# Swapping q and k on ScalarE, and the rows of 1/rms by a transpose through DRAM, in a one-core hybrid layer

## The chip, the cores and the metric

The kernel runs on one core of one Trainium2 chip. The metric is the device time of one execution in microseconds (us); the median of several executions counts. The engines are TensorE (PE, matmuls), VectorE (DVE, elementwise), ScalarE (ACT, activations and copies), GpSimd (POOL, not used here) and SyncE (SP), whose queue issues nearly all transfers (DMA).

## The reference

One layer over 1024 positions of width 1024, in float32. Cut to what matters here:

```
h = rms_norm(x, norm1_w)                       # x * 1/rms(x) per position, times a weight per channel
q, k, v, g_ret, x_lru, y_lru, gate_ret, gate_lru = split(h @ w_in)
q, k = rotary(q), rotary(k) * dk**-0.5         # 4 heads of 128; halves (x1, x2) ->
                                               #   (x1 cos - x2 sin, x1 sin + x2 cos)
o    = chunkwise_retention(q, k, v)            # decayed attention per chunk, state across chunks
y_a  = (head_group_norm(o) * silu(g_ret)) @ w_ret_o
y_b  = (rg_lru(conv(x_lru)) * gelu(y_lru)) @ w_lru_o
x    = x + (sigmoid(gate_ret) * y_a + sigmoid(gate_lru) * y_b) @ w_out
h    = rms_norm(x, norm2_w)
gate, val = split(h @ ffn_w_up)
x    = x + (gelu(conv(gate)) * val) @ ffn_w_down
out  = rms_norm(x, norm_f_w)
```

## The kernel before

All large products run on PE as 128 by 128 by 512 matmuls. Each float32 operand is split into a high part (a cast on ScalarE, L771) and a low part (a subtraction on VectorE, L772), and three products of the parts are added up. Most products of two 1024-wide matrices go through a fast scheme with seven block products in place of eight (`mm_fast`): three PSUM banks X, Y, Z take twelve matmuls per block product (L898), and between the block products ScalarE copies banks (L905, L919) and VectorE adds them up (L910). Twelve matmuls after a bank is full PE may need it again.

The layer runs in stages on PE: the values of all heads first (L1500), then 20 products of the input projection in the order of `SEQ` (gates, y, heads, x), then the output projections of both branches, `w_out` (`out_job`), 24 products of the gated MLP (`up_job`), and `w_dn` in three groups (`down_job`). Activations lie transposed: channels on partitions, positions along the free dimension.

**Retention.** When the product that makes q and k of a head is done, `rotary_head` and `retention_head` are queued behind it as side work that is woven into the next products. `rotary_head` holds k or q as `t`, 128 partitions (channels of the head) by 1024 positions. Rotation needs each channel's partner 64 partitions away: two transfers (L1318, L1319) write the upper half of `t` to the lower half of `w` (tile `qs`) and the lower half to the upper. Then VectorE makes `t*cos` (L1320), `w*sin` (L1321) and the sum (L1323). Keys are then transposed through DRAM (L1327 to L1335). `retention_head` makes per block of 128 positions the scores (L1356), the masked scores times values (L1363), the state's part (L1362) and the state's update (L1370), all on PE in plain float32.

**Rows of 1/rms.** The sum of squares is made per position with positions on partitions: eight columns of 128 positions. `rstd_of` makes 1/rms of them (128 by 8). Since activations lie transposed, 1/rms is needed along the free dimension, on all partitions: the tile `rowt` (128 by 1024). `rows_of` makes it: VectorE scales the identity by a column (L1083), PE multiplies a matrix of ones with that diagonal (L1084), four such per PSUM bank, and ScalarE copies the bank to half of `rowt` (L1085). It is called twice: at the start for the first norm, where `rescale` (L1095) multiplies the input with the row, and after `w_out` for the second norm, where `with_row` (L1416) multiplies each result of an up product with it.

**The order of the work.** All operations are first recorded. A planner then runs through them with a table of costs (`cost`, `forward`), picks for each engine what to run next, and gives tiles their places in SBUF. `side` marks PE work to be woven in, `within(slack, side)` gives a due time. Operations get a random bias from `SEED`; the planner goes through several `ROUNDS`, in each of which it brings forward what held up PE (`blame`), and keeps the order with the shortest planned span. `emit` writes each engine's instructions in that order, so every engine runs a fixed sequence and waits in it. Transfers are planned with a landing time from `TILE` and `LAND`.

Of the kernel before, what the change touches and what calls it, by code (L numbers as in the profile page):

```python
# [17 lines left out]
ALU = mybir.AluOpType  # L18

P = 128  # L20
D = 1024
T = 1024
KT = 8
# [240 lines left out]
class Prog:  # L264
# [378 lines left out]
    EAGER = 12000  # L643
    EARLY = 20000
    FETCH = 24000
    SEED, JITTER, ROUNDS, STALL, URGE = 19, 400.0, 6, 150.0, 6000.0
    BEGIN = 400
    TILE = 800.0
    LAND = 1900.0
# [8 lines left out]
    def emit(self, engines, make, behind):  # L658
        at, sent = {}, []
        for o in self.order:  # L660
# [16 lines left out]

SMALL = (("par", (P, NPAR)), ("cst", (P, NCONST)), ("st", (P, 16)), ("nst", (P, 7, 8)), ("lt", (P, 2, 8)),
         ("state0", (P, 256)), ("state1", (P, 256)), ("bst", (P, 4, 6)),
         ("mv", (P, 4, 2)), ("rs", (P, 3, 4)), ("rowt", (P, T)))  # L680
SPILL = (("og", (KT, P, T)), ("u", (KT, P, T)), ("y", (KT, P, T)), ("sg", (2, KT, P, T)), ("t1", (KT, P, T)),
         ("x1", (T, D)), ("td", (3, 4, 2, P, 2, TH)), ("to", (2, 4, 2, P, 2, TH)), ("ff", (3, 8, P, 2, 4, P)), ("rot", (4, P, T)),
         ("ss", (12, 2, P, T)), ("v", (2, KT, P, TH)),
         ("kt", (HEADS, 2, 4, P, P)), ("ot", (HEADS, 2, 4, P, 2, P)))
# [21 lines left out]
TSLACK = 8000.0  # L706
# [24 lines left out]
def record(prog, fx):  # L731
    V, S, G, PE, SY = (Engine(prog, n) for n in ("DVE", "ACT", "POOL", "PE", "SP"))
    par, cst, st, nst, lt = (fx[n] for n in ("par", "cst", "st", "nst", "lt"))
    rst, bst, mv, rs = fx["rst"], fx["bst"], fx["mv"], fx["rs"]
    og_d, u_d, y_d, sg_d, t1_d, x1_d, td_d, to_d, ff_d, rot_d, ss_d, v_d, kt_d, ot_d = (
        fx[n + "_d"] for n in ("og", "u", "y", "sg", "t1", "x1", "td", "to", "ff", "rot", "ss", "v", "kt", "ot"))
    x, positions, normf, w_in, w_v, w_ro, w_lo, w_out, w_up, w_dn, w_gate, out, xt = (
        fx[n] for n in ("x", "positions", "normf", "w_in", "w_v", "w_ro", "w_lo", "w_out", "w_up", "w_dn", "w_gate", "out", "xt"))
    ident = cst[:, C_ID:C_ID + P]

    def get(name, shape=(P, TH), dt=F32):
        return Ref(VT("u", shape, dt, name))

    def sm():
        return Ref(VT("sm", (P, P), F32, "sc"))

    def bank(kind="g"):
        return Ref(VT(kind, (P, TH), F32, kind))

    def pc(name, i):  # L750
        return par[:, PCOL[name] + i:PCOL[name] + i + 1]

    def cut(t, h):
        if h is None:
            return t
        return t[:, h] if len(t.shape) == 3 else t[:, TH * h:TH * h + TH]
# [4 lines left out]
    @contextmanager  # L761
    def within(slack, side=False):
        was = prog.slack, prog.side
        prog.slack, prog.side = slack, side
        yield
        prog.slack, prog.side = was

    def split(src, name, here=False):
        hi = get(name + "h", src.shape, F32R)
        lo = src.alias(F32R) if here else get(name + "l", src.shape, F32R)  # L770
        S.copy(hi, src)  # L771
        V.tensor_sub(lo, src, hi.bitcast(F32))  # L772
        return hi, lo
# [228 lines left out]
    def put(op, name, jp, made):  # L1002
        for i in range(2):
            op[name, 2 * jp + i] = made[0][:, i], made[1][:, i]
# [65 lines left out]
            V.scalar_tensor_tensor(t2, t2, -1.0, b21, ALU.mult, ALU.subtract)  # L1070
            put(op, "T4", jp, split(t2, "b", True))

    row = {0: fx["rowt"]}

    def rows_of(r, side, slack=1000.0):
        one = sm()
        V.memset(one, 1.0)
        for h in range(2):
            with within(slack, side):
                ps = bank()  # L1080
                for t in range(4):
                    dg = sm()
                    V.tensor_scalar(dg, ident, r[:, 4 * h + t:4 * h + t + 1], None, ALU.mult)  # L1083
                    PE.matmul(ps[:, 128 * t:128 * t + 128], one, dg, start=True, stop=True)  # L1084
                S.copy(cut(row[0], h), ps)  # L1085

    def scaled_split(t, w, name):
        hi, lo = get(name + "h", t.shape, F32R), get(name + "l", t.shape, F32R)
# [4 lines left out]
    def rescale(q, ch, name):  # L1093
        t = q[ch // 2][:, ch % 2]
        V.scalar_tensor_tensor(t, t, pc(name, ch), row[0].rearrange("p (h c) -> p h c", h=2), ALU.mult, ALU.mult)  # L1095

    def start_transposed():
        if UNI:
            q = {(kh, h, jp): get("xq", PAIR) for h in range(2) for kh in range(2) for jp in range(2)}
            for h in range(2):  # L1100
                for k in range(KT):
                    t = q[k // 4, h, k % 4 // 2][:, k % 2]
                    SY.dma_start(t, xt[h, k])
                    S.activation(t, t, AF.Copy, scale=pc("norm1_w", k))
                    b = f"B{k // 4 + 1}{h + 1}"
                    if b != "B12" or STD_L:
                        h1[b, k % 4] = split(t, "h")
            for jp in range(2):
                b11, b12, b21, b22 = (q[kh, h, jp] for kh in range(2) for h in range(2))
                V.tensor_sub(b11, b11, b12)  # L1110
                V.tensor_sub(b12, b22, b12)
                V.scalar_tensor_tensor(b22, b11, -1.0, b22, ALU.mult, ALU.subtract)
                V.scalar_tensor_tensor(b21, b22, -1.0, b21, ALU.mult, ALU.subtract)
                for n, t in (("T1", b11), ("T2", b22), ("T3", b12), ("T4", b21)):
                    put(h1, n, jp, split(t, "b", True))
        q = [get("xq", QUAD) for _ in range(0 if UNI else 4)]
        for h in range(0 if UNI else 2):
            for k in range(KT):
                t = q[k // 2][:, k % 2, h]
                SY.dma_start(t, xt[h, k])  # L1120
                h1u[f"B{k // 4 + 1}{h + 1}", k % 4] = scaled_split(t, pc("norm1_w", k), "h")
        prog.floor = FLOOR1
        for t in range(8):
            b = get("xs", FLAT)
            SY.dma_start(b, x[128 * t:128 * t + 128, :])
            S.activation(b, b, AF.Square, accum_out=nst[:, 0, t:t + 1])
        a, r, w = (nst[:, i, 0:8] for i in range(3))
        V.tensor_scalar(a, a, 1.0 / D, EPS, ALU.mult, ALU.add)
        rstd_of(r, a, w)
        rows_of(r, True)  # L1130
        if not UNI:
            for k in (0, 1, 4, 5, 2, 3, 6, 7):
                rescale(q, k, "norm1_w")
            operand(h1, of_quads(q), ("B11", "B21", "B22"), False)
            tsets(h1, of_quads(q))
        prog.floor = -1e9
# [173 lines left out]
    def rotary_head(hd, qk):  # L1310
        for m in range(2):
            if m == 0 or UNI:
                tab = [get("rt", FLAT) for _ in range(2)]
                for i in range(2):
                    SY.dma_start(tab[i], rot_d[2 * m + i])
            t = qk[m]
            w = get("qs", FLAT)
            SY.dma_start(w[0:64, :], t[64:128, :])  # L1318
            SY.dma_start(w[64:128, :], t[0:64, :])  # L1319
            V.tensor_mul(t, t, tab[0])  # L1320
            V.tensor_mul(w, w, tab[1])  # L1321
            yield 1.8
            V.tensor_add(t, t, w)  # L1323
            yield 1.8
        for h in range(2):
            t = get("kx")
            V.transpose(t.view(lambda a: a.rearrange("p (c b j) -> p c b j", c=4, b=4)),  # L1327
                        cut(qk[1], h).view(lambda a: a.rearrange("p (b c j) -> p c b j", b=4, c=4)))
            SY.dma_start(kt_d[hd, h].rearrange("c p r -> p c r"), t.rearrange("p (c r) -> p c r", c=4))
            yield 0.9  # L1330
            t, kd[h] = get("kl"), get("kd")
            for c in range(4):
                SY.dma_start(t[32 * c:32 * c + 32].rearrange("i (a r) -> i a r", a=4),
                             kt_d[hd, h, c].rearrange("(a i) r -> i a r", a=4))
            S.activation(kd[h].rearrange("p (b a j) -> p b a j", a=4, b=4), t.rearrange("p (a b j) -> p b a j", a=4, b=4),  # L1335
                         AF.Copy, scale=cst[:, C_KDEC + hd:C_KDEC + hd + 1])
            yield 0.5
# [102 lines left out]
    og, u = {}, {}  # L1440
# [86 lines left out]
    for what in SEQ.split():  # L1527
        if what == "g":
            w, n = gates.pop(0)
            to = store(lambda m, w=w, n=n: sg_d[w, 2 * n + m])  # L1530
# [5 lines left out]
        elif what[0] == "y":  # L1536
            n = int(what[1])
            to = store(lambda m, n=n: y_d[2 * n + m])
# [4 lines left out]
        elif what[0] == "x":  # L1543
            n = int(what[1])
# [9 lines left out]
    one, ps = warm = sm(), bank()  # L1554
# [3 lines left out]
        PE.matmul(ps[:, 0:P], one, one, start=True, stop=True)  # L1558
    prog.side = False
    V.memset(st, 1.0)  # L1560
    S.activation(st[:, 0:1], st[:, 1:2], AF.Sqrt)
    prog.hold = 14000.0
    SY.dma_start(par[:, 8:NPAR], fx["params"][:, 8:NPAR])
# [150 lines left out]
    for h in range(2):  # L1714
# [10 lines left out]
        with within(TSLACK, True):  # L1725
            a, b, c, e = (nst[:, i, 4 * h:4 * h + 4] for i in range(4))
            v, r = nst[:, 5, 4 * h:4 * h + 4], nst[:, 4, 4 * h:4 * h + 4]
# [5 lines left out]
                V.tensor_add(v, v, e)  # L1733
            V.tensor_scalar(v, a if RELOAD else v, 1.0 / D, EPS, ALU.mult, ALU.add)
            rstd_of(r, v, a)
    rows_of(nst[:, 4, :], True, max(1000.0, TSLACK))
    if UNU:
        pass
    elif UNS:
# [3 lines left out]
    else:  # L1743
        for h in range(2):
            for k in range(KT):
                t = x1q[k // 2][:, k % 2, h]
# [109 lines left out]
def tile_trunk_layer(ctx, tc, x, positions, params, consts, normf, w_in, w_v, w_ro, w_lo,  # L1856
# [9 lines left out]
    fx["rst"] = [fx.pop("state0"), fx.pop("state1")]  # L1866
    for n, shape in SPILL:
        fx[n + "_d"] = Ref(Fixed(pdr.tile(list(shape), F32, tag=n, name=n + "_d"), shape))
# [83 lines left out]
```

## Time and profile before

| | us |
|---|---|
| three runs | 1582.25, 1582.71, 1580.74 |
| median | 1582.25 |
| the profiled execution, in all | 1582.89 |
| its span | 1581.1 |
| PE busy in the span | 1567.7 |

The profile comes from one execution. Its span runs from the first to the last instruction; the time of the execution is 1.8 us longer. Instructions are named by engine, line of the kernel and tile ("out<-in"). The end of a matmul is modelled and overlaps the next one, so its time on PE is best read as the distance from one start to the next. "[1.24 <-DVE ub L1323]" behind an instruction means that its engine stood idle for 1.24 us before it, and that the instruction on L1323 of VectorE ended this wait.

### The profile page before, as it was taken

Reading aid. Unit: us, or ns where it says so; the run is one execution under the profiler, and the core shown is the slowest. Engines: PE = TensorE matmul, PEld = TensorE weight load, DVE = VectorE, ACT = ScalarE, POOL = GpSimd, SP = SyncE. Lnnn points to the kernel's source line nnn. Section 1 sums busy time; section 2 is a strip of 40 time slices with the busy share of each in tenths; the row PEclk is TensorE's granted clock in tenths of the full one; section 3 lists DMA queues with packets and bytes.
Section 4 is the critical chain, followed back from the end, with each engine's and each line's share of the span. In section 5 each row is a group of like instructions: output and inputs, shape, how many; then the busy total and the mean of one; then the engine's idle time right before and its main releaser. Section 6 shows DMA issues by size and latency. Waiting matters only on the chain.

```text
span 1581.1 us, 19113 instructions
## 1 busy us (share of the span) xinstructions
PE 1567.7 (99%) x6988; PEld 1297.5 (82%) x6988; DVE 1280.9 (81%) x1725; ACT 868.5 (55%) x1171; POOL 0.2 (0%) x4
## 2 busy tenths in 40 slices
PE   9999999999999999999999999999999999999998
PEld 7888888788888888888888888888888888888886
DVE  4996877887888988978795887788888788877795
ACT  7464458476458458645456854444444445454463
POOL 0000000000000000000000000000000000000000
PEclk9999999999999999999999999999999999999999
DMA  9414445457487868959353522456655335776752
GB/s 328 143 65 154 118 157 167 147 178 255 118 296 240 271 209 303 393 205 363 122 178 124 183 80 81 133 187 200 200 195 200 138 100 175 281 269 264 274 198 78
DMA packets 146013, 307.09 MB, mean 194 GB/s; under 512 B 11264, under 2 KB 60544, under 8 KB 145920
## 3 DMA queue, kind: packets, MB, share of 16 engines
q1 hardware_dynamic: 145488, 305.35, 56.4%
q8 instruction: 55, 0.90, 0.2%
q10 hardware_dynamic: 432, 0.53, 0.1%
q14 instruction: 38, 0.31, 0.1%
HBM read 208.31 MB, written 93.32 MB: 191 GB/s over the span
## 4 chain that ended last, share of the span: by engine, by line
PE 91%; DMA 4%; DVE 3%; ACT 1%; issue 1%; SPq 1%; DVEq 0%; ACTq 0%
PE g L898 82%; PE g L1500 4%; PE a L1275 3%; DMA xq<-xt 1%; DMA qs<-ub 1%; PE a L1363 1%; PE a L1362 1%; PE a L1370 1%; DMA qs<-ua 1%; DMA xs<-x 1%; DVE qs L1321 1%; PE a L1680 0%; PE a L1356 0%; DVE wl L772 0%; DVE ub L1323 0%
## 5 line engine op out<-in xcount | busy, mean ns | idle before, releaser
L898 PE MATMUL g<-bh,wh 128*128 128x512 f32 x1728 | 676.0, 391 | 0.6 <-DVE ub L910 0.6
L898 PEld LDWEIGHTS g<-bh,wh 128*128 128x128 f32 x1728 | 324.5, 188 | 68.1 <-DVE ub L910 1.5
L898 PE MATMUL g<-bh,wl 128*128 128x512 f32 x880 | 344.5, 391 | 0.0
L898 PE MATMUL g<-bl,wh 128*128 128x512 f32 x864 | 339.5, 393 | 0.0
L898 PE MATMUL g<-bh,wrr 128*128 128x512 f32 x824 | 321.6, 390 | 0.0
L771 ACT CAST wh<-wr 128x1024 fp32r<-128x1024 f32 (+1 forms) x220 | 198.1, 917 | 102.2 <-PE g L898 28.5
L898 PEld LDWEIGHTS g<-bh,wl 128*128 128x128 f32 x880 | 165.3, 188 | 33.9
L898 PEld LDWEIGHTS g<-bl,wh 128*128 128x128 f32 x864 | 162.3, 188 | 32.9
L772 DVE TENSOR_TENSOR wrr<-wr,wh 128x1024 fp32r<-128x1024 f32 (+1 forms) x154 | 152.0, 990 | 37.5 <-ACT wh L771 37.4
L898 PEld LDWEIGHTS g<-bh,wrr 128*128 128x128 f32 x824 | 154.7, 188 | 31.8
L898 PE MATMUL g<-tdr,wh 128*128 128x512 f32 x320 | 124.5, 389 | 0.0
L771 ACT CAST wh<-ws 128x1024 fp32r<-128x1024 f32 x66 | 69.2, 1049 | 82.6 <-PE g L898 47.0
L898 PE MATMUL g<-hl,wh 128*128 128x512 f32 x288 | 112.2, 390 | 0.0
L898 PE MATMUL g<-hh,wh 128*128 128x512 f32 x288 | 112.1, 389 | 0.0
L910 DVE TENSOR_TENSOR ub<-ub,g 128x512 f32<-128x512 f32 x72 | 49.2, 683 | 53.0 <-PE g L898 52.9
L905 ACT ACTIVATE ub<-g 128x512 f32<-128x512 f32 x72 | 42.8, 596 | 84.0 <-PE g L898 75.6
L772 DVE TENSOR_TENSOR wl<-ws,wh 128x1024 fp32r<-128x1024 f32 x66 | 80.4, 1219 | 9.8 <-PE g L898 9.5
L772 DVE TENSOR_TENSOR wl<-wr,wh 128x1024 fp32r<-128x1024 f32 x66 | 80.3, 1217 | 7.6 <-ACT wh L771 2.7
L898 PE MATMUL g<-tsr,wh 128*128 128x512 f32 x208 | 81.2, 390 | 0.0
L919 ACT ACTIVATE g<-g 128x512 f32<-128x512 f32 x72 | 42.0, 584 | 61.1 <-PE g L898 60.9
L905 ACT ACTIVATE ua<-g 128x512 f32<-128x512 f32 x72 | 43.0, 598 | 56.3 <-PE g L898 52.2
L910 DVE TENSOR_TENSOR ua<-ua,g 128x512 f32<-128x512 f32 x72 | 49.2, 683 | 29.2 <-PE g L898 28.4
(265 smaller groups left out, 2539.1 us busy)
## 6 DMA issues: line engine op xcount, KB each, us to landing
wr<-w_up SPq DMA_DIRECT2D x50, 512.0 KB, 4.5
wr<-w_in SPq DMA_DIRECT2D x48, 512.0 KB, 4.5
dw<-w_dn SPq DMA_DIRECT2D x42, 512.0 KB, 4.6
ff_d<-gc SPq DMA_DIRECT2D x24, 512.0 KB, 3.8
wr<-ff_d SPq DMA_DIRECT2D x24, 512.0 KB, 6.9
td<-td_d SPq DMA_DIRECT2D x24, 512.0 KB, 7.2
x<-x_d SPq DMA_DIRECT2D x24, 512.0 KB, 6.8
td_d<-dw SPq DMA_DIRECT2D x18, 512.0 KB, 5.7
```

What stands on the lines that cost most here:

```text
L771: S.copy(hi, src)
L772: V.tensor_sub(lo, src, hi.bitcast(F32))
L898: PE.matmul(ps, (hi, lo)[a][:, c], o[b], start=first and n == 0, stop=n == 11, skip_group_check=True)
L905: S.activation(cut(d[m], h), ps, AF.Copy, scale=scale)
L910: (V.tensor_sub if m else V.tensor_add)(u, u, ps)
L919: S.activation(Y, X, AF.Copy)
L1275: PE.matmul(ps, wg[a][:, g, cs], xs[b][:, k], start=q == 0, stop=q == 5)
L1321: V.tensor_mul(w, w, tab[1])
L1362: PE.matmul(p2[:, 0:256], q[:, bs], rst[cur], start=True, stop=False)
L1363: PE.matmul(p2[:, 0:256], s, v, start=first, stop=True)
L1370: made.append(PE.matmul(p3[:, 0:256], kd[h][:, bs], v, start=True, stop=True))
L1500: PE.matmul(ps[t], a[i][:, 128 * t:128 * t + 128], b[j], start=k == 0 and i + j == 0, stop=k == KT - 1 and i == 1)
```

## The change

`rotary_head` makes the swapped tile by two copies on ScalarE, each of 64 partitions by 1024, in place of two transfers, and gives back control to the weaving once more. `rows_of` no longer uses PE: VectorE copies 1/rms into the first eight columns of a 128 by 32 tile (`rcol`, whose other columns are zeroed once at the start), transposes it in blocks of 32 by 32 into `rrow`, four transfers store eight rows each of 32 values to a row in DRAM, and one transfer reads that row back to all 128 partitions of `rowt`. Two small tiles and one DRAM buffer are new. The planner gets another seed and one more round.

```diff
-    SEED, JITTER, ROUNDS, STALL, URGE = 19, 400.0, 6, 150.0, 6000.0
+    SEED, JITTER, ROUNDS, STALL, URGE = 6, 400.0, 7, 150.0, 6000.0
...
-         ("mv", (P, 4, 2)), ("rs", (P, 3, 4)), ("rowt", (P, T)))
+         ("mv", (P, 4, 2)), ("rs", (P, 3, 4)), ("rowt", (P, T)),
+         ("rcol", (P, 2, 32)), ("rrow", (P, 2, 32)))
...
-    def rows_of(r, side, slack=1000.0):
-        one = sm()
-        V.memset(one, 1.0)
-        for h in range(2):
-            with within(slack, side):
-                ps = bank()
-                for t in range(4):
-                    dg = sm()
-                    V.tensor_scalar(dg, ident, r[:, 4 * h + t:4 * h + t + 1], None, ALU.mult)
-                    PE.matmul(ps[:, 128 * t:128 * t + 128], one, dg, start=True, stop=True)
-                S.copy(cut(row[0], h), ps)
+    def rows_of(r, side, at):
+        with within(None, side):
+            V.tensor_copy(rcol[:, at, 0:8], r)
+            V.transpose(rrow[:, at], rcol[:, at])
+            for a in range(4):
+                SY.dma_start(row_d[at].view(lambda d, a=a: d.rearrange("o (t a j) -> a (o t) j", a=4, j=32)[a], T // 4),
+                             rrow[32 * a:32 * a + 8, at])
+            SY.dma_start(row[0], row_d[at].to_broadcast((P, T)))
...
-        rows_of(r, True)
+        rows_of(r, True, 0)
...
             w = get("qs", FLAT)
-            SY.dma_start(w[0:64, :], t[64:128, :])
-            SY.dma_start(w[64:128, :], t[0:64, :])
+            S.copy(w[0:64, :], t[64:128, :])
+            S.copy(w[64:128, :], t[0:64, :])
+            yield 1.0
             V.tensor_mul(t, t, tab[0])
             V.tensor_mul(w, w, tab[1])
...
+    V.memset(rcol, 0.0)
...
-    rows_of(nst[:, 4, :], True, max(1000.0, TSLACK))
+    rows_of(nst[:, 4, :], True, 1)
```

More of the change, by code (lines that the diff above doesn't have):

```diff
@@ L679 @@
          ("state0", (P, 256)), ("state1", (P, 256)), ("bst", (P, 4, 6)),
-         ("mv", (P, 4, 2)), ("rs", (P, 3, 4)), ("rowt", (P, T)))
-SPILL = (("og", (KT, P, T)), ("u", (KT, P, T)), ("y", (KT, P, T)), ("sg", (2, KT, P, T)), ("t1", (KT, P, T)),
+         ("mv", (P, 4, 2)), ("rs", (P, 3, 4)), ("rowt", (P, T)),
+         ("rcol", (P, 2, 32)), ("rrow", (P, 2, 32)))
+SPILL = (("row", (2, 1, T)), ("og", (KT, P, T)), ("u", (KT, P, T)), ("y", (KT, P, T)), ("sg", (2, KT, P, T)), ("t1", (KT, P, T)),
          ("x1", (T, D)), ("td", (3, 4, 2, P, 2, TH)), ("to", (2, 4, 2, P, 2, TH)), ("ff", (3, 8, P, 2, 4, P)), ("rot", (4, P, T)),
@@ L734, in record @@
     rst, bst, mv, rs = fx["rst"], fx["bst"], fx["mv"], fx["rs"]
-    og_d, u_d, y_d, sg_d, t1_d, x1_d, td_d, to_d, ff_d, rot_d, ss_d, v_d, kt_d, ot_d = (
-        fx[n + "_d"] for n in ("og", "u", "y", "sg", "t1", "x1", "td", "to", "ff", "rot", "ss", "v", "kt", "ot"))
+    row_d, og_d, u_d, y_d, sg_d, t1_d, x1_d, td_d, to_d, ff_d, rot_d, ss_d, v_d, kt_d, ot_d = (
+        fx[n + "_d"] for n in ("row", "og", "u", "y", "sg", "t1", "x1", "td", "to", "ff", "rot", "ss", "v", "kt", "ot"))
     x, positions, normf, w_in, w_v, w_ro, w_lo, w_out, w_up, w_dn, w_gate, out, xt = (
@@ L1071, in tsets @@
             put(op, "T4", jp, split(t2, "b", True))
-    row = {0: fx["rowt"]}
-    def rows_of(r, side, slack=1000.0):
-        one = sm()
-        V.memset(one, 1.0)
-        for h in range(2):
-            with within(slack, side):
-                ps = bank()
-                for t in range(4):
-                    dg = sm()
-                    V.tensor_scalar(dg, ident, r[:, 4 * h + t:4 * h + t + 1], None, ALU.mult)
-                    PE.matmul(ps[:, 128 * t:128 * t + 128], one, dg, start=True, stop=True)
-                S.copy(cut(row[0], h), ps)
+    row, rcol, rrow = {0: fx["rowt"]}, fx["rcol"], fx["rrow"]
+    def rows_of(r, side, at):
[6 more added lines that the diff above has]
+            SY.dma_start(row[0], row_d[at].to_broadcast((P, T)))
     def scaled_split(t, w, name):
```

## The prediction

> **What bounds the kernel now.** First the page: its head and the busy shares.
>
> ```profile
> span 1581.1 us, 19113 instructions
> PE 1567.7 (99%) x6988; PEld 1297.5 (82%) x6988; DVE 1280.9 (81%) x1725; ACT 868.5 (55%) x1171; POOL 0.2 (0%) x4
> ```
>
> TensorE (PE) is busy 99% of the span, so the end is set by how many matmuls it has and by the few places where it stands. A busy share hides small gaps, because the end of each matmul is modelled; therefore I go on with the windows (columns: stretch, then PE, PEld, DVE, ACT, POOL busy, granted clock, DMA share, GB/s).
>
> ```profile
> 41.00:97.00 56.00, 56.00 (x249) 46.37 (x248) 54.28 (x64) 26.93 (x33) 0.00 (x0) 1.00 0.27 94
> 154.00:200.00 46.00, 45.82 (x212) 38.18 (x211) 36.38 (x79) 21.34 (x35) 0.00 (x0) 1.00 0.49 129
> 272.00:313.00 41.00, 39.63 (x182) 32.55 (x181) 36.77 (x69) 18.72 (x30) 0.00 (x0) 1.00 0.53 151
> 387.00:440.00 53.00, 51.76 (x238) 42.97 (x237) 44.65 (x89) 22.37 (x36) 0.00 (x0) 1.00 0.53 154
> 511.00:562.00 51.00, 50.15 (x229) 41.50 (x229) 46.27 (x82) 21.53 (x34) 0.00 (x0) 1.00 0.78 259
> 608.00:822.00 214.00, 214.00 (x946) 177.24 (x945) 187.06 (x212) 120.41 (x146) 0.00 (x0) 1.00 0.72 268
> 920.00:1574.00 654.00, 654.00 (x2886) 541.47 (x2884) 526.37 (x623) 312.94 (x416) 0.00 (x0) 1.00 0.52 181
> ```
>
> From 608 to 822 and from 920 to 1574 us PE has no gap at all and the clock is full: 654.00/2886 = 0.227 us per matmul of 512 columns. Nothing can be gained there; a new order of work can only lose. The four short windows are those of the four retention heads, and there PE is missing 0.18, 1.37, 1.24 and 0.85 us. Who it waits for stands in the view of waits, PE alone (total, times, longest):
>
> ```profile
> PE a L1356 <- DVE ua L1323: 1.4, 3, 1.0
> PE a L1356 <- DVE ub L1323: 1.2, 1, 1.2
> PE a L1680 <- DVE x1q L1620: 0.8, 1, 0.8
> PE g L898 <- DVE ub L910: 0.6, 1, 0.6
> ```
>
> L1356 is the first score matmul of each head, and L1323 the last step of the rotation of k or q, behind the swap. So the swap stands on the path that sets the end, but only through 2.6 us of waits.
>
> **The matmuls that go.** Two calls of `rows_of` make eight diagonal matmuls each (L1084). What one costs is read from the starts in PE's timeline:
>
> ```profile
> 912.22 0.39 PE L898 MATMUL g<-hh,wrr 128*128 128x512 f32 x1
> 912.44 0.39 PE L898 MATMUL g<-hh,wh 128*128 128x512 f32 x1
> ...
> 913.12 0.40 PE L898 MATMUL g<-hh,wh 128*128 128x512 f32 x1
> 913.36 0.83 PE L1084 MATMUL g<-sc,sc 128*128 128x128 f32 x6
> 913.94 0.48 PE L898 MATMUL g<-hl,wh 128*128 128x512 f32 x1
> 914.26 0.39 PE L898 MATMUL g<-hh,wrr 128*128 128x512 f32 x1
> ```
>
> Each L1084 matmul is two records, so "x6" is three. From 913.12 to 914.26 pass 1.14 us, in which two ordinary matmuls would take 0.45; the rest, 0.69, is three diagonal ones with the way in and out, 0.23 each. All 16 make 16 x 0.23 = **3.7 us**, on the path, since PE is full on both sides. With less lost in changing over it would be 3.4, with single ones 0.26 each, so 4.2: those are the bounds. Their 16 scalings on VectorE and four copies on ScalarE go too; neither ends a wait of PE in the rows above, so they count nothing.
>
> **The swap.** Sixteen transfers go; sixteen ScalarE copies of 64 partitions by 1024 come. First what the transfers cost:
>
> ```profile
> 404.34 0.39 PE L898 MATMUL g<-bl,wh 128*128 128x512 f32 x1
> 405.97 0.71 PE L1356 MATMUL a<-ua,ub 128*128 128x128 f32 x4 [1.24 <-DVE ub L1323]
> ...
> 532.08 0.71 PE L1356 MATMUL a<-ua,ub 128*128 128x128 f32 x4 [0.30 <-DVE ua L1323]
> ```
>
> ```profile
> 520.46 1.23 DVE L1321 TENSOR_TENSOR qs<-qs,rt 128x1024 f32<-128x1024 f32 x1 [2.62 <-DMA qs<-ua]
> ...
> 527.35 0.68 DVE L910 TENSOR_TENSOR ub<-ub,g 128x512 f32<-128x512 f32 x1
> ```
>
> ```profile
> DMA to landing us min/median/max: 3.1/6.7/8.7
> ```
>
> The last row is the view of tile qs: a swap lands 6.7 us after its issue. VectorE works in a fixed order, stands 2.62 us at 520 for it, and the late L910 behind it is the fourth PE wait above (0.6). Waits shown as 1.24 are longer from start to start: 405.97 - 404.34 - 0.23 = 1.40, so 0.16 is hidden in each. Swap-related loss: 1.4 + 1.2 + 0.6 + 5 x 0.16 = **4.0 us** in five stalls.
>
> A copy on ScalarE is priced by the nearest cast of 1024 columns:
>
> ```profile
> L771 ACT CAST wh<-ws 128x1024 fp32r<-128x1024 f32 x66 | 69.2, 1049 | 82.6 <-PE g L898 47.0
> L919 ACT ACTIVATE g<-g 128x512 f32<-128x512 f32 x72 | 42.0, 584 | 61.1 <-PE g L898 60.9
> ```
>
> 1.05 us, half the partitions or not; between 0.53 (if halves cost half) and 1.05 I take 1.05. A pair is 2.1 us in place of 6.7, so a rotated tensor is ready some 4.6 us sooner, and SP's queue loses 16 issues, which stood ahead of weight and value loads. In the four head windows ScalarE gets 4.2 us more on 21.34 of 46, 18.72 of 41, 22.37 of 53 and 21.53 of 51: over 20 us stay free in each, and that is the cover at which I price the copies at nothing.
>
> How much of the 4.0 goes? The planner that writes the order will place the scores earlier as well, because it knows the copies' length. What is then late next is VectorE: three operations of 1.2 us for each of q and k, among weight splits. The wait of 0.30 at 532 follows such a chain. I let one stall of that kind stay per head, 4 x 0.4 = 1.6, and take **-2.4**. Bounds: -4.0 (all gone) and 0 (what is late next takes their place).
>
> **The rows through DRAM.** New at each call: a copy and a 32-wide transpose on VectorE, four small stores, and, after them, one load of 4 KB to all 128 partitions, 512 KB, all on SP's queue.
>
> ```profile
> kt_d<-kx SPq DMA_DIRECT2D x8, 256.0 KB, 2.8
> rt<-rot_d SPq DMA_DIRECT2D x8, 512.0 KB, 3.7
> nf<-normf SPq DMA_DIRECT2D x1, 512.0 KB, 8.6
> ```
>
> ```profile
> 45.53 2.48 DVE L1095 SCALAR_TENSOR_TENSOR xq<-xq,par,rowt 128x1024 f32<-128x1024 f32 x2
> ```
>
> ```profile
> 909.07 0.15 DVE L1000 TENSOR_TENSOR nst<-nst 128x4 f32<-128x4 f32 x1
> ...
> 918.27 1.23 DVE L1416 TENSOR_TENSOR ua<-ua,rowt 128x1024 f32<-128x1024 f32 x1 [1.24 <-ACT rowt L1085]
> ...
> 922.01 0.68 DVE L910 TENSOR_TENSOR ua<-ua,g 128x512 f32<-128x512 f32 x1
> ```
>
> ```profile
> 35.35 0.16 DVE L1000 TENSOR_TENSOR nst<-nst 128x8 f32<-128x8 f32 x1
> ```
>
> ```profile
> 914.22 0.80 SPq L786 DMA_DIRECT2D wr<-w_up  x2
> ```
>
> Second call: 1/rms is ready at 909.2; 0.5 for copy and transpose (an estimate from 0.15 for small operations), four issues of 0.40 = 1.6, the store 2.8 and an issue 0.4 give 914.5. The load then takes 3.7 (same size, plain) or 8.6 (same shape, but one sample): the row lands between 918.2 and 923.1, against its first use at 918.27. So VectorE stands 0 to 4.8 us in front of L1416, and behind it wait L910, which frees a bank for PE, the gate convolution (L1756) and weight splits. PE needs the bank of L910 no sooner than twelve matmuls after it is full, 12 x 0.227 = 2.7 us. On PE that is 0 to 2.1; I take 0.5, nearer the lower end because the load of the same size is the median of eight. On SP the next issue is the load at 914.22, just when the row's load would go: no delay. First call: 35.5 + 0.5 + 1.6 + 2.8 + 0.4 + 3.7 to 8.6 = 44.5 to 49.4, against 45.53. VectorE may stand 3.9 us there, but that is covered:
>
> ```profile
> 97.02 62.57 PE g L898 x276
> ```
>
> ```profile
> 137.75 1.11 SPq L1226 DMA_DIRECT2D rot_d<-rot  x2
> ```
>
> The first products with scaled operands start at 97 (chain of waits), and VectorE's filler until then, the rotary tables, is stored only at 137 (SP's timeline). So 0 is taken, and 3.9 if that cover is gone.
>
> The Trainium skill, page "DMA: Bandwidth & Descriptors", section "Anatomy of one DMA", gives another price and speaks against a way through DRAM: about 2.0 us fixed for each transfer, most of it the receipt of the write, worst where the target is DRAM, and two here stand in series. It is measured on the other kind of queue. The 2.8 above agrees in kind. By its formula the store is 2.0 and the load 3.2 (estimates), the row would be there at 916.9, nothing would wait, and the sum below would be 0.5 lower.
>
> **The other order.** A new seed and one more round of the planner give every engine another order and every tile another place. The stall at L1680 (0.8 shown, 0.94 from start to start) may go: lower bound -0.9. Upper bound: a new stall like the largest, 1.4, in four places, +5.6. No row shows it; I take +0.3, near nothing, since PE is gapless for 868 us in the two long windows with the same kinds of work.
>
> **Sum.** -3.7 - 2.4 + 0.5 + 0.3 = **-5.3 us**. The profiled execution has a span of 1581.1 and took 1582.89 in all; it would be 1577.6. It lies 0.64 above the median of the three runs, 1582.25, so for the median **1577.0**.
>
> **The rivals.**
>
> *All swap stalls go and the row is in time.* For it: 4.6 us sooner is over three times the longest stall, 1.4. Against it: VectorE is 80% busy. 1582.25 - 3.7 - 4.0 = 1574.5. Chance 0.2.
>
> *A wait in place of the one removed.* The keys still go through DRAM for their transpose, 2.8 us and a load behind it, and scores start earlier; PE then stands for the decayed keys or for VectorE as long as now. Only the matmuls go: 1582.25 - 3.7 + 0.5 + 0.3 = 1579.4, with one more 1.4 stall 1580.8. For it: the stalls are named by VectorE, not by the transfer. Chance 0.26.
>
> *ScalarE blocks the bank evictions: slower.* The copies stand in ScalarE's order between evictions such as L919, whose bank PE needs 2.7 us later. A pair of copies and an eviction are 2.1 + 0.58 = 2.7: it just fits. The same stretch also has a table load:
>
> ```profile
> 162.95 1.28 ACT L1234 ACT_TABLE_LOAD   x1
> ```
>
> Where both come ahead of an eviction PE stands about 1.2 us; in all eight pairs that is 9.9: 1582.25 - 3.7 - 2.4 + 9.9 = 1586.1. It decides for slower once all eight pairs are hit (over 6.1 + 3.2 = 9.3), or six of them if the -2.4 isn't had. For it: copies wait for VectorE's L910, in order. Against it: ScalarE is under half busy there and the planner knows all durations. Chance 0.12; some 0.02 is left for new stalls of the order alone.
>
> *The change does not do what it says:* a swap across partitions by copies may run slower than the cast, up to twice (2.1 each). Still a pair of 4.2 lies under 6.7; this falls into the second rival.
>
> **Chances and range.** Forecast 0.40. A measurement of this kernel can tell about 0.2%, 3.2 us: faster is below 1579.1, slower above 1585.4. The forecast counts 0.34 faster and 0.06 same; the first rival 0.2 faster; the second 0.08 faster, 0.18 same; the third 0.02 same and 0.10 slower, the rest 0.02 slower: faster 0.62, same 0.26, slower 0.12. The lower bounds together give 1582.25 - 4.2 - 4.0 - 0.9 = 1573.1; I go to 1572.5. Upwards the second rival with a late row (+1.6 more) and two new stalls (2.8) is 1579.4 + 4.4 = 1583.8; I go to 1585, which leaves out most of the third.
>
> **What would show it.** Right: no diagonal matmuls, 32 PE records fewer; the waits of the first score matmuls fall from 2.6 us to about 1; copies near 1.05 us; VectorE's wait for the row before its first use near 919 under 3 us. Wrong: PE waits for decayed keys or for evictions in the head windows, any PE gap between 608 and 822 or after 920, or a row that lands after 921 with PE standing behind it.

## The result, and the profile after

| | us |
|---|---|
| before, median of 5 runs (1580.74 to 1582.71) | 1581.66 |
| changed, median of 5 runs (1574.05 to 1575.58) | 1574.87 |
| ratio | 0.9956, interval 0.9942 to 0.9971 |
| the profiled execution: in all, and its span | 1574.89, 1573.1 |

The changed kernel is 6.8 us faster (0.44%; by the interval between 4.6 and 9.2). The forecast was 5.3 us less than before, 1577.0 against 1574.87 measured. The two profiled executions lie 8.0 us apart, because the one of before (1582.89) was longer than each of these five.

The head of the page after, the first lines of parts 1 and 4 among it (the latter is the chain that ended last, by engine):

```profile
span 1573.1 us, 19066 instructions
PE 1563.2 (99%) x6956; PEld 1295.1 (82%) x6956; DVE 1278.3 (81%) x1712; ACT 883.9 (56%) x1181; POOL 0.2 (0%) x4
...
PE 96%; DMA 2%; DVE 1%; ACT 1%; issue 0%; SPq 0%; DVEq 0%; ACTq 0%
```

PE has 32 records less, the 16 diagonal matmuls. ScalarE works 15.4 us longer than the 868.5 of before. The windows of the changed kernel, the columns as before:

```profile
154.00:200.00 46.00, 46.00 (x214) 38.73 (x213) 39.17 (x82) 23.38 (x37) 0.00 (x0) 1.00 0.35 98
...
272.00:313.00 41.00, 41.00 (x192) 34.56 (x191) 37.63 (x74) 23.52 (x36) 0.00 (x0) 1.00 0.37 112
...
387.00:440.00 53.00, 53.00 (x245) 44.41 (x244) 44.27 (x89) 28.04 (x42) 0.00 (x0) 1.00 0.48 153
...
511.00:562.00 51.00, 50.76 (x234) 42.32 (x233) 46.72 (x92) 25.66 (x40) 0.00 (x0) 1.00 0.64 204
...
608.00:822.00 214.00, 214.00 (x945) 176.88 (x944) 182.82 (x208) 113.45 (x137) 0.00 (x0) 1.00 0.71 259
...
920.00:1566.00 646.00, 645.95 (x2850) 534.53 (x2848) 521.79 (x618) 311.60 (x410) 0.00 (x0) 1.00 0.54 183
```

In the four head windows PE misses 0.24 us in place of 0.18 + 1.37 + 1.24 + 0.85 = 3.64. The two long windows are as full as before (0.05 us is missing in the second). PE's waits after (total, times, longest):

```profile
PE g L1557 <- DVE sc L1554: 1.0, 1, 1.0
PE a L1273 <- ACT li L1275: 0.7, 1, 0.7
PE a L1680 <- DVE x1q L1620: 0.3, 1, 0.3
PE g L1499 <- ACT hh L1087: 0.3, 1, 0.3
PE g L899 <- DVE wrr L773: 0.3, 1, 0.3
PE a L1369 <- ACT kd L1334: 0.2, 1, 0.2
```

The first score matmul (L1355 now) is not in the list at all. A wait in the recurrent block has grown (0.7, before 0.2), and new are one of 0.3 for a weight split (L773) and one of 0.2 for the decayed keys, which the prediction had named as a sign against it, though far smaller than what went.

### The profile page after: what moved, and what is told of

It reads as the page before. It is cut to its first block, busy times and chain, and to the rows that moved or that the text cites. A ratio compares the mean times of both kernels' runs of the same rounds, so it can differ in the third digit from the quotient of the medians.

```text
span 1573.1 us, 19066 instructions
## 1 busy us (share of the span) xinstructions
PE 1563.2 (99%) x6956; PEld 1295.1 (82%) x6956; DVE 1278.3 (81%) x1712; ACT 883.9 (56%) x1181; POOL 0.2 (0%) x4
## 4 chain that ended last, share of the span: by engine, by line
PE 96%; DMA 2%; DVE 1%; ACT 1%; issue 0%; SPq 0%; DVEq 0%; ACTq 0%
PE g L899 84%; PE g L1499 6%; PE a L1273 2%; PE a L1362 1%; PE a L1369 1%; PE a L1361 1%; DMA wgr<-w_gate 1%; PE a L1355 0%; DMA bf<-og_d 0%; PE a L1680 0%; DMA oc<-ot_d 0%; DMA kl<-kt_d 0%; DMA xq<-xt 0%; DVE bf L1017 0%; DVE wrr L773 0%
## 5 line engine op out<-in xcount | busy, mean ns | idle before, releaser
L899 PE MATMUL g<-bh,wh 128*128 128x512 f32 x1728 | 676.2, 391 | 0.0
L899 PEld LDWEIGHTS g<-bh,wh 128*128 128x128 f32 x1728 | 324.5, 188 | 66.2 <-ACT g L920 0.4
L899 PE MATMUL g<-bh,wl 128*128 128x512 f32 x880 | 345.7, 393 | 0.0
L899 PE MATMUL g<-bl,wh 128*128 128x512 f32 x864 | 338.7, 392 | 0.0
L899 PE MATMUL g<-bh,wrr 128*128 128x512 f32 x824 | 321.5, 390 | 0.0
L899 PEld LDWEIGHTS g<-bh,wl 128*128 128x128 f32 x880 | 165.2, 188 | 33.9
L899 PEld LDWEIGHTS g<-bl,wh 128*128 128x128 f32 x864 | 162.3, 188 | 33.1
L899 PEld LDWEIGHTS g<-bh,wrr 128*128 128x128 f32 x824 | 154.7, 188 | 32.0
L773 DVE TENSOR_TENSOR wrr<-wr,wh 128x1024 fp32r<-128x1024 f32 (+1 forms) x154 | 152.4, 992 | 35.2 <-ACT wh L772 35.1
L899 PE MATMUL g<-tdr,wh 128*128 128x512 f32 x320 | 124.5, 389 | 0.0
L899 PE MATMUL g<-hl,wh 128*128 128x512 f32 x288 | 112.1, 389 | 0.0
L899 PE MATMUL g<-hh,wh 128*128 128x512 f32 x288 | 112.1, 389 | 0.0
L911 DVE TENSOR_TENSOR ub<-ub,g 128x512 f32<-128x512 f32 x72 | 49.4, 686 | 66.1 <-PE g L899 65.9
L773 DVE TENSOR_TENSOR wl<-wr,wh 128x1024 fp32r<-128x1024 f32 x66 | 80.5, 1219 | 8.1 <-ACT wh L772 2.7
L773 DVE TENSOR_TENSOR wl<-ws,wh 128x1024 fp32r<-128x1024 f32 x66 | 80.5, 1220 | 6.0 <-PE g L899 3.9
L899 PE MATMUL g<-tsr,wh 128*128 128x512 f32 x208 | 81.0, 390 | 0.0
L899 PEld LDWEIGHTS g<-tdr,wh 128*128 128x128 f32 x320 | 60.1, 188 | 12.5
```

The costliest lines, as they stand in the source:

```text
L899: PE.matmul(ps, (hi, lo)[a][:, c], o[b], start=first and n == 0, stop=n == 11, skip_group_check=True)
L911: (V.tensor_sub if m else V.tensor_add)(u, u, ps)
```

## The experiments

Any edit makes the planner find another order for the whole kernel, and that alone can move the time. So the first four experiments and the sixth keep the order and the places of one of the two kernels: the planner works as before, and only what is issued for an operation is exchanged. The others let it plan anew. The hook of the first kind, in `emit`:

```diff
+            if o.alt is not None:
+                at[o.line](getattr(engines[o.alt[0]], o.alt[1]), args, kw)
+                continue
             inst = at[o.line](getattr(real, o.how), args, kw)
+            if o.twice:
+                at[o.line](getattr(real, o.how), args, kw)
```

All ratios are to the kernel before (1581.8 to 1581.9 in these comparisons).

### The swap alone, in the old order

```diff
-            SY.dma_start(w[0:64, :], t[64:128, :])
-            SY.dma_start(w[64:128, :], t[0:64, :])
+            for o in (SY.dma_start(w[0:64, :], t[64:128, :]), SY.dma_start(w[64:128, :], t[0:64, :])):
+                o.alt = "ACT", "copy"
```

> The kernel before with its planned order and places kept as they are; only the sixteen swaps are issued as ScalarE copies, at the places in the order where the transfers stood. Theory (the swaps' late landing makes the stalls at the first scores): PE's waits at the first score matmuls, 2.6 us before, fall to under 0.5 and the time by 3 to 4 us. Rival (VectorE or the keys are late anyway): under 1 us. Second rival (copies that the order did not foresee hold up ScalarE's evictions): new waits of PE for ScalarE, gain under 2 us or a loss.

Measured: 1579.32, ratio 0.9981 (0.9972 to 0.9990), 2.6 us less. PE's waits, the second to the fifth line of the view:

```profile
PE a L1685 <- DVE x1q L1625: 0.8, 1, 0.8
PE a L1361 <- DVE ub L1328: 0.7, 1, 0.7
PE a L1367 <- ACT ob L1372: 0.6, 1, 0.6
PE g L903 <- ACT g L924: 0.5, 1, 0.5
```

The waits at the first scores (L1361 here) fall from 2.6 to 0.7 us, and a wait of 0.5 for an eviction (L924) is new. So the theory's mechanism holds, and the time falls clear of the first rival (under 1 us); but it fell by less than the 3 to 4 us that the theory gave, for 0.7 stays at the scores, where it gave under 0.5, and a little of the second rival is real: both pairs of copies of the last head stand ahead of that eviction, as ScalarE's timeline shows.

```profile
509.34 2.11 ACT L1323 COPY qs<-ua 64x1024 f32<-64x1024 f32 x2
511.35 2.10 ACT L1323 COPY qs<-ub 64x1024 f32<-64x1024 f32 x2
513.48 0.62 ACT L776 CAST wh<-wr 128x512 fp32r<-128x512 f32 x1
514.00 0.58 ACT L924 ACTIVATE g<-g 128x512 f32<-128x512 f32 x1
```

The planner had left no room for these copies, and yet 16.8 us more on ScalarE made PE's waits for ScalarE only 0.7 us longer in all (1.5 in place of 0.8 in the views of waits): ScalarE's idle time did take them.

### The transfers back, in the new order

```diff
-            S.copy(w[0:64, :], t[64:128, :])
-            S.copy(w[64:128, :], t[0:64, :])
+            for o in (S.copy(w[0:64, :], t[64:128, :]), S.copy(w[64:128, :], t[0:64, :])):
+                o.alt = "SP", "dma_start"
```

> The changed kernel with its order and places kept; only the sixteen copies are issued as transfers on SP's queue, at their places in the order. Theory: swaps land some 4.6 us later than this order allows for, VectorE stands before the rotation and PE at the first scores; at least the 4.0 us of before come back, and up to 4 x 4.6 = 18 us. Rival (the new order alone brought the gain): within 1 us of the changed kernel.

Measured: 1592.86, ratio 1.0064 (1.0047 to 1.0080): 18 us above the changed kernel. VectorE's and PE's timelines in the third head:

```profile
399.06 1.22 DVE L1324 TENSOR_TENSOR ua<-ua,rt 128x1024 f32<-128x1024 f32 x1 [5.65 <-DMA qs<-ua]
```

```profile
403.49 0.39 PE L904 MATMUL g<-bh,wl 128*128 128x512 f32 x1
407.28 0.49 PE L1360 MATMUL a<-ua,ub 128*128 128x128 f32 x2 [3.40 <-DVE ub L1327]
```

VectorE stands 5.65 us for the swap, and PE 3.40 for VectorE. The order that counts on copies cannot do with transfers; the new order alone did not bring the gain. Not all of the 18 us is waiting: the granted clock of two stretches (160 to 180 us and 520 to 540) is 0.91 in place of 1.00, of which more below. The transfers also hold up what stands behind them on SP's queue; that share was not separated.

### The diagonal matmuls twice

```diff
-                    PE.matmul(ps[:, 128 * t:128 * t + 128], one, dg, start=True, stop=True)
+                    PE.matmul(ps[:, 128 * t:128 * t + 128], one, dg, start=True, stop=True).twice = True
```

> The kernel before with its order and places kept; each of the 16 diagonal matmuls is issued twice in a row. Theory (PE is full on both sides, the work counts in full): a second one in a row costs 0.19 us, as three in a row take 0.58 from start to start, so 3.1 us more. Rival (PE has hidden slack at the start, where it waits for the split inputs): only the eight of the second call count, 1.6 us more. No effect would mean that their removal brought nothing.

Measured: 1586.02, ratio 1.0025 (1.0016 to 1.0035), 4.1 us more; the spans differ by 3.9. PE's timeline, to be compared with the three diagonal matmuls of the prediction:

```profile
915.52 1.50 PE L1089 MATMUL g<-sc,sc 128*128 128x128 f32 x12
916.77 0.48 PE L903 MATMUL g<-hl,wh 128*128 128x512 f32 x1
```

Six take 1.25 us where three took 0.58: 0.22 for each further one, where 0.19 was expected, so 3.6 for 16. They count in full at both calls; the rival with slack at the start (1.6) falls.

### The copies twice, in the new order

```diff
-            S.copy(w[0:64, :], t[64:128, :])
-            S.copy(w[64:128, :], t[0:64, :])
+            for o in (S.copy(w[0:64, :], t[64:128, :]), S.copy(w[64:128, :], t[0:64, :])):
+                o.twice = True
```

> The changed kernel with its order and places kept; each of the sixteen copies is issued twice in a row, 16.8 us more on ScalarE and 2.1 us more latency per swapped tensor. Theory (ScalarE has cover): under 1.5 us more, and what there is comes at the first scores. Rival (ScalarE's order is tight, a pair just fits before an eviction): 1.2 us or more at each of eight pairs, near 10 us, with PE waiting for evictions.

Measured: 1593.68, ratio 1.0073 (1.0054 to 1.0091); the span is 17.7 us longer than that of the changed kernel. The third head, ScalarE and PE:

```profile
401.53 4.26 ACT L1321 COPY qs<-ub 64x1024 f32<-64x1024 f32 x4
405.70 0.57 ACT L925 ACTIVATE g<-g 128x512 f32<-128x512 f32 x1
```

```profile
403.14 0.39 PE L904 MATMUL g<-bh,wl 128*128 128x512 f32 x1
406.32 0.50 PE L904 MATMUL g<-bh,wh 128*128 128x512 f32 x1 [2.79 <-ACT g L925]
```

and the same place in the changed kernel, ScalarE and the matmul that stood there:

```profile
388.32 1.05 ACT L1316 COPY qs<-ub 64x1024 f32<-64x1024 f32 x1
389.38 1.05 ACT L1317 COPY qs<-ub 64x1024 f32<-64x1024 f32 x1
390.33 0.57 ACT L920 ACTIVATE g<-g 128x512 f32<-128x512 f32 x1
```

```profile
392.28 0.39 PE L899 MATMUL g<-bh,wh 128*128 128x512 f32 x1
```

In the changed kernel the eviction follows the copies at once and ends at 390.90, 1.4 us before that matmul starts, at 392.28. Both pairs of this head stand ahead of it, so doubling puts 4.2 us in front of it, and 4.2 - 1.4 = 2.8 is what PE then stands. So the theory of cover fell: ScalarE is idle half of the time in these windows, but in front of this eviction it has 1.4 us to spare.

That the span grew by about as much as the copies is a coincidence, though. PE's waits add up to 12.5 us in place of 2.8: 9.7 more, nearly all at one place in each head, and close to the rival's 10 for eight pairs. The windows of three of these places, and PE's timeline at the second one, show what the rival did not count:

```profile
160.00:180.00 20.00, 17.58 (x71) 13.70 (x71) 15.20 (x22) 11.73 (x14) 0.00 (x0) 0.91 0.53 145
280.00:300.00 20.00, 17.16 (x69) 13.75 (x68) 15.28 (x16) 14.11 (x17) 0.00 (x0) 0.91 0.42 133
520.00:540.00 20.00, 18.15 (x73) 14.50 (x73) 15.70 (x19) 14.76 (x17) 0.00 (x0) 0.91 0.50 160
```

```profile
289.58 0.80 PE L904 MATMUL g<-bh,wh 128*128 128x512 f32 x1 [2.84 <-ACT ua L911]
290.17 0.63 PE L904 MATMUL g<-bl,wh 128*128 128x512 f32 x1
290.60 0.63 PE L904 MATMUL g<-bh,wrr 128*128 128x512 f32 x1
```

The granted clock is 0.91 there, where the changed kernel has 1.00, and a matmul takes 0.43 us from start to start in place of 0.227. By the clock that is 20 x 0.09 = 1.8 us in each window, some 5 in all. Behind the wait of 2.79 at 406 the clock stays at 1.00, so a wait of this length does not always bring it down. Waits and clock make 15 of the 17.7 us; of the rest, 1.2 us is there 15 us after the start, before any copy. So this kernel's waits say that some 7 of the 16.8 us were hidden, and its time alone would say none.

### The copies twice, planned

The two copies stand in a loop of two in `rotary_head`, in the changed kernel; seed and rounds stay.

> The changed kernel with each copy recorded twice, so that the planner places them, same seed and rounds. In the fixed order the same 16.8 us cost 18 us. Theory (the copies are free only because the planner leaves room for them in ScalarE's order; ScalarE as such has time): under 5 us more than the changed kernel, up to 1580. Rival (ScalarE has no time in the head stages at all): 12 us or more, 1587 or above.

Measured: 1581.29, ratio 0.9997 (0.9987 to 1.0006), 6.4 us above the changed kernel: a little more than the theory allowed, far less than the rival's 12. Where the planner knows the 16.8 us, the time grows by 6.4. That is the price of this order, not of ScalarE alone: PE's longest wait in it, 2.2 us, is for VectorE at 889, far behind the heads.

### The row's load twice

```diff
-            SY.dma_start(row[0], row_d[at].to_broadcast((P, T)))
+            SY.dma_start(row[0], row_d[at].to_broadcast((P, T))).twice = True
```

> The changed kernel with its order and places kept; the load of the row to all partitions is issued twice in a row at both calls, so the row is there some 4 us later and SP's queue stands as long. Theory (the row has cover at both calls, by the rotary tables and by the earlier 1/rms): within 1 us of the changed kernel. Rival (VectorE in front of the first use of the row holds PE): 2 us or more, with a wait of PE after 918 for VectorE.

Measured: 1574.67, ratio 0.9955 (0.9940 to 0.9970), the time of the changed kernel. VectorE's timeline at the two first uses of the row:

```profile
61.62 7.26 DVE L1098 SCALAR_TENSOR_TENSOR xq<-xq,par,rowt 128x1024 f32<-128x1024 f32 x6 [2.60 <-DMA rowt<-row_d]
```

```profile
917.65 1.23 DVE L1420 TENSOR_TENSOR ua<-ua,rowt 128x1024 f32<-128x1024 f32 x1 [1.09 <-DMA rowt<-row_d]
```

VectorE stands 2.60 and 1.09 us, and PE has no wait after 918: both calls have cover, and with a single load VectorE does not wait at the second one at all.

### Other orders

One part at a time, or only the seed, planned anew. In the seed line the numbers 19 and 6 rounds are those of before, 6 and 7 rounds those of the changed kernel.

```diff
-    SEED, JITTER, ROUNDS, STALL, URGE = 19, 400.0, 6, 150.0, 6000.0
+    SEED, JITTER, ROUNDS, STALL, URGE = 6, 400.0, 7, 150.0, 6000.0
```

> The kernel before with the changed kernel's seed and rounds, planned anew: the order alone. Theory (the two parts make the gain, 4 us by the diagonals and 2.6 by the swaps in an unchanged order; the seed only scatters): 1577 to 1587, with PE's diagonals there and waits at the first scores again. Rival (the seed makes the gain): about 1575.

> The changed kernel with the seed and rounds of before, planned anew. Theory: 1573 to 1578, no wait of PE over 0.5 us at the first scores. Rival (the seed makes the gain): about 1581.

> Only the swaps by ScalarE, rows still by PE; planned anew with the new seed and rounds. Theory: the share of the swaps, 2 to 4 us below before: 1577 to 1580, the diagonals still there. Rival (the parts work only together, or the order decides): outside 1575 to 1582.

> Only the swaps by ScalarE, as in the run before, with the seed and rounds of before. Theory: again 2 to 4 us below before; the distance to the run with the other seed shows how far the order alone moves the time, at most 3 us.

> Only the rows through DRAM, swaps still by transfers; planned anew with the new seed and rounds. Theory: the share of the diagonals, 3 to 5 us below before, 1577 to 1579, with PE's waits at the first scores as before (2 to 4 us). Rival (the order decides): outside 1575 to 1582.

| median us, ratio with interval | seed of before | seed of the change |
|---|---|---|
| old parts | 1581.9 (before) | 1588.74, 1.0043 (1.0028 to 1.0058) |
| rows by DRAM only | not run | 1582.27, 1.0006 (0.9997 to 1.0015) |
| swaps by ScalarE only | 1579.27, 0.9985 (0.9975 to 0.9994) | 1577.76, 0.9975 (0.9966 to 0.9985) |
| both parts | 1575.36, 0.9956 (0.9940 to 0.9973) | 1574.87, 0.9956 (0.9942 to 0.9971) |

The seed is not the gain: with the old parts the new seed loses 6.9 us, slower than the 1587 that I had given it at most, and with the new parts the old seed gives the same time within 0.5. Rows only missed its expectation of 1577 to 1579 and lies, by 0.3, where its rival put it (the order decides). Down the columns, the rows are worth 1577.76 - 1574.87 = 2.9 and 1579.27 - 1575.36 = 3.9 where the copies are in, and 6.5 where they are not; the swaps are worth 2.6 and 11.0 with the rows by PE, and 7.4 with the rows by DRAM. With transfers the time hangs on the order (1581.9 and 1588.7); with copies two orders differ by 1.5 and 0.5. The swaps alone come to the same time in the old order (1579.32), without the additional `yield`, and planned anew with the old seed and the `yield` (1579.27); so with this seed the new order and the `yield` together bring nothing. Where the orders with transfers lose is in the view of waits. Old parts with the new seed, PE, first two lines, and VectorE's timeline:

```profile
PE g L898 <- DVE wl L772: 2.9, 3, 1.2
PE g L898 <- DVE ub L910: 2.5, 1, 2.5
```

```profile
526.44 1.23 DVE L1321 TENSOR_TENSOR qs<-qs,rt 128x1024 f32<-128x1024 f32 x1 [3.83 <-DMA qs<-ub]
...
528.72 0.68 DVE L910 TENSOR_TENSOR ub<-ub,g 128x512 f32<-128x512 f32 x1
```

and rows only, PE:

```profile
PE g L899 <- DMA to_d<-bf: 1.8, 1, 1.8
PE a L1354 <- DVE ub L1321: 1.1, 1, 1.1
...
PE a L1354 <- DVE ua L1321: 0.9, 1, 0.9
```

In the first, VectorE stands 3.83 us for a swap, and L910, which adds up a bank, comes late behind it: the pattern of before at 520, longer. In the second the waits at the first scores are there as before, 2.0, and one of 1.8, put down to another transfer (`to_d<-bf`), is new at the last head. In both profiles the granted clock is 0.91 from 520 to 540 us, which is some 1.8 us of each by the reckoning above. The long L910 wait of the first and the score waits of the second stand behind swaps; that the rest of the loss comes from the swaps was not tried. Nor was another table of costs: `forward` counts 0.7 + 0.8 + 1.9 = 3.4 us for a swap in an empty queue, against 6.7 measured at the median, and whether an order planned with the longer time would do as well with transfers is open.

### Another seed for the changed kernel

```diff
-    SEED, JITTER, ROUNDS, STALL, URGE = 6, 400.0, 7, 150.0, 6000.0
+    SEED, JITTER, ROUNDS, STALL, URGE = 23, 400.0, 9, 150.0, 6000.0
```

> The changed kernel with seed 23 and nine rounds, the order with the shortest span in the planner's own reckoning among some forty seeds. Theory (the order only scatters by 2 us or so about the parts' gain, and PE's remaining gaps are some 8 us, 3.5 of them at the start): 1571 to 1576. Rival (the seed of the changed kernel is itself a lucky one): 1577 or above.

Measured: 1573.30 (1572.81 to 1573.73), ratio 0.9948 (0.9932 to 0.9965). It is the fastest of all kernels here, 1.6 us under the changed one by the medians; the intervals of the two ratios overlap.

## Why the prediction was right

**The direction, and the bound, held.** PE sets the end, and both what was taken off it and what it had waited for came out of the time. In fixed orders the parts measure 2.6 (swap) and about 3.6 to 4.1 (diagonals, by doubling them), together 6.2 to 6.7 of the 6.8. The diagonals were doubled and not taken out in a fixed order; in orders planned anew, taking them out brought 2.9 and 3.9 beside copies.

**The matmuls that go, -3.7: held.** Doubling gives 3.6 by PE's timeline and 4.1 by the time.

**The swap, -2.4: right in size (2.6 in the old order), with one step wrong for the changed kernel.** I let one stall of 0.4 per head stay, on the ground that VectorE's chain would be late next. In the old order 0.7 does stay at the scores. In the changed kernel no wait at the first scores is left, as the first rival had it. But not all of that rival's 4.0 shows in the time: the 6.8 less the 3.6 to 4.1 of the diagonals leave 2.7 to 3.2 for the swap and the order together, since other waits grew (0.7 at L1273, 0.3 at L899, 0.2 at L1369). So "late next" is the step that was off: what was late next was not the chain at the scores, and it cost about 1 us and not 1.6. What the profile shows is the first rival, all swap stalls gone and the row in time, and its 1574.5 lies nearer to the 1574.87 than the forecast's 1577.0; 0.6 of the distance is that the median of before fell from 1582.25 to 1581.66 with two more runs.

**The cover of the copies: the price held, the reason was too coarse.** I priced the copies at nothing because over 20 us of each head window are free on ScalarE; in the second window it is 41 - 18.72 - 4.2 = 18.1. In the old order, which left no room for them, the idle time did take the sixteen copies, for 0.7 us of new waits. In the changed order a second sixteen made PE stand 9.7 us more. What counts is the time to spare in front of the next eviction, 1.4 us at the one that was followed, and not the idle share of the window. The third rival's mechanism is real, and a single pair per tensor stays clear of it in both orders but for that one wait of 0.5.

**The rows through DRAM, +0.5: nothing.** VectorE did not wait for the row at 918. Three things differ from my reckoning. In the new order 1/rms is ready ten microseconds earlier (it is copied at 898.62, where it was ready at 909.2 before), the four stores do not go one behind the other, and the load takes the lower of my two bounds. VectorE and SP's queue in the changed kernel, and SP's queue in the kernel with two loads:

```profile
898.62 0.17 DVE L1078 COPY rcol<-nst 128x8 f32<-128x8 f32 x1
...
916.86 1.22 DVE L1415 TENSOR_TENSOR ua<-ua,rowt 128x1024 f32<-128x1024 f32 x1
```

```profile
900.56 6.25 SPq L787 DMA_DIRECT2D wr<-w_up  x2
906.85 0.33 SPq L1081 DMA_DIRECT2D row_d<-rrow  x1
910.02 0.33 SPq L1083 DMA_DIRECT2D rowt<-row_d  x1
```

```profile
910.11 3.96 SPq L1088 DMA_DIRECT2D rowt<-row_d  x2
```

Two weight loads hold up SP's queue for 6.25 us ahead of the last store, where I had allowed for four issues in a row, 1.6 in all. That the row was still in time is luck: 1/rms came earlier by more than this. The last store is issued at 906.85, and the load, which waits for it, at 910.02: 3.2 us, as I had it (2.8 + 0.4). Two loads in series run from 910.11 to 917.65, where VectorE starts: 3.8 each, and not the 8.6 of the one sample of that shape. The Trainium skill, page "DMA: Bandwidth & Descriptors", section "Anatomy of one DMA", gives 2.0 and, worked out from its formula, 3.2 as estimates. Both legs are longer here (3.2 and 3.8). Its consequence, no wait at the second call, came true, but with 1/rms ten microseconds early the runs do not test it. At the first call the row was later than both my bounds, 44.5 and 49.4: the stores stand between other transfers on SP's queue, the load is issued only at 54.28, and the first use is at 59.8 in place of 45.53. VectorE does not wait, since it has other work until then, and PE stays full until 154 all the same; so the cover was right and the reckoning of the time was not.

**The other order, +0.3: its width was too small.** The four planned orders with copies in the table lie within 1574.9 to 1579.3, parts included; but the old parts under the new seed lose 6.9 us, more than the upper bound of 5.6 that I gave for new stalls. The lowered clock, which I had left out, is some 1.8 of the 6.9.

## What to carry to other kernels

The idle share of an engine that runs a fixed order does not say how much more it can take: ask what stands right behind the new instruction, by when that must be done, and double the instruction in the same order to see. Then look at the waits and at the granted clock, since the whole difference in time can resemble the added work by chance. With transfers, which landed 3.1 to 8.7 us after their issue, the two orders tried differed by 6.9 us; with copies of 1.05 us, by 1.5 and 0.5. A change and the order that comes with it are told apart by keeping one of them fixed.

## What the runs showed of the hardware

A copy on ScalarE over 64 partitions by 1024 float32, from one half of the partitions to the other, takes 1.05 us:

```profile
L1316 ACT COPY qs<-ub x4: 1049/1050/1051, 152.5 to 508.7; 64x1024 f32<-64x1024 f32 x4
```

That is what the cast of 128 partitions by 1024 takes (1049 ns): half the partitions and the crossing together change nothing here. A copy of 64 partitions that stays in its half was not run.

After some waits of PE, not all, the granted clock fell: behind the wait of 2.84 us in the kernel with doubled copies, matmuls took 0.43 us from start to start in place of 0.227 until 292.7, and the clock of that window was 0.91; behind the wait of 2.79 us in the same kernel it stayed at 1.00.
